# A down projection in block products, and transposes of merged sums with one PSUM bank per pair

## The chip, the cores and the metric

The kernel runs on one core of one Trainium2 chip. The metric is device time in microseconds (us), the median of three runs. Engines are called as the profile calls them: PE (TensorE, matrix products), PEld (its weight loads), DVE (VectorE), ACT (ScalarE), POOL (GpSimd), SP (the queue that issues most DMAs).

## The reference

One layer of a decoder trunk on 256 tokens of width 2048, in float32: a hybrid mixer with a residual, a SwiGLU with a residual, a last norm.

```
m   = g0*(ya @ w_br_a) + g1*(yb @ w_br_b) + g2*(yc @ w_br_c)      # three mixers, gated
h   = x + m @ w_out
f   = rms_norm(h, norm_ffn)
h   = h + (silu(f @ w_gate) * (f @ w_up)) @ w_down                # D_FF = 5632
out = rms_norm(h, norm_final)
```

## The kernel before

Every product is taken in three parts of type float32r. `split` (L105 to L112) cuts a float32 tile into a high part, which ACT writes (L108), and the low remainder, which DVE subtracts (L109). A product is then hi\*hi + lo\*hi + hi\*lo: three matmuls of 128x512. All weights pass through that split on the chip, so every matmul needs one ACT and one DVE pass over its weights first.

Tokens are two tiles of 128 (NT = 2), weights are loaded as 1 MB `raw` tiles. A `Group` (units of class `KTiles`) makes 512 output columns over K in steps of four K-tiles: 24 matmuls a unit. A `Squares` group makes two blocks of 512 columns at once, from pairs of K-tiles. A pair of kind "N" takes eight products (24 matmuls). A pair of kind "W" takes seven (21 matmuls) by a scheme of block sums: its unit "Wp" has 9 matmuls, its unit "Ws" 12, and it needs sums of the weight blocks (L433 to L435 on DVE, into one more slot) and differences of the activation blocks (`differences`, L152 to L173). Seven banks collect the products (numbered 1 to 7): `squares_early` (L455) reads banks 1, 6 and 7 when the last "Ws" is through, `squares_end` (L463 to L471) the others at the end.

SwiGLU has 11 chunks of 512 columns of D_FF, grouped in `PARTS` of 3, 3, 3 and 2. For each chunk `swiglu` runs one `Squares` group (K-pairs of kinds NNWNWNWN, gate and up as the two blocks). Its `finish` takes the results out of PSUM, applies silu (ACT, L941), multiplies (DVE, L944), transposes on PE (L951, four 128x128 into one bank, twice a chunk) and splits the result. After a part, `down` multiplies its 12 (or 8) K-tiles with w_down, one `Group` for each 512 output columns, and adds onto `h` (L986).

The program's order is the order in which the code is written (manual schedule). `run` walks the units. Ahead of a unit it issues the cuts of later units, as long as the slots that these need (N 2, Wp 3, Ws 2) stay within `cap` (9 in these stages); then the unit's matmuls; then one step of a side generator (`beside`): those are `finish`, the transposes and so on. So an engine's queue holds cuts and side steps in one fixed order, and an instruction whose input is late holds up all behind it on its engine. Tiles live in 22 `slots` of 8 KB a partition and in 8 PSUM banks; a new tile waits until its slot or bank was last read.

In the mixer, `br` merges the three gated branches into `m`; its `turn` transposes `m` by `transposed` (L246: two transposes into a bank of their own, one split of 128x256), two calls a step.

Of the kernel before, what the change touches and what calls it, by code (L numbers as in the profile page):

```python
# [13 lines left out]
OP = mybir.AluOpType  # L14
# [19 lines left out]
PARTS = ((0, 3), (3, 6), (6, 9), (9, 11))  # L34
FFN_KINDS = "NNWNWNWN"
GATE_KINDS = "NWNWNWWN"


def bucket_spans():
# [12 lines left out]
def trunk(ctx: ExitStack, tc: tile.TileContext, x, norm_mix, norm_ffn, w_in, w_pool, pool_scale,  # L52
# [64 lines left out]
    class Lazily(dict):  # L117


        def __init__(self, make):  # L120
            self.make = make
# [5 lines left out]
    class Halves:  # L127

        def __init__(self, kinds=None):
# [18 lines left out]
        def differences(self, p, a):  # L150

            e = wk().rearrange("p (n s) -> p n s", s=P)  # L152
            n = 4 if self.kinds[p] == "W" else 2
            if n == 2:
                nc.vector.tensor_tensor(e[:, 0:2], a[:, :, 0], a[:, :, 1], OP.subtract)
            else:
                f = a.rearrange("p k t s -> p (k t) s")
                nc.vector.tensor_tensor(e[:, 0:2], f[:, 1:2].to_broadcast([P, 2, P]), f[:, 0:4:3], OP.subtract)
                nc.vector.tensor_tensor(e[:, 2], f[:, 0], e[:, 1], OP.subtract)
                nc.vector.tensor_tensor(e[:, 3], f[:, 2], e[:, 2], OP.subtract)  # L160
            for i, (tile, used) in enumerate(self.tiles):
                if used + 2 * n <= 16:
                    break
            else:
                i, tile, used = len(self.tiles), late_slot([16, P], F32R), 0
# [11 lines left out]
        def fill(self, p, pt, scales):  # L177

            a = wk()
            for j in range(2):  # L180
                k = slice(j * SEQ, (j + 1) * SEQ)
                nc.scalar.activation(a[:, k], pt[:, k], AF.Copy, scale=scales[j])
            split(*self.pair(p), a.rearrange("p (k s) -> p k s", k=2))
            self.differences(p, a.rearrange("p (k t s) -> p k t s", k=2, t=NT))


    xt = [slot([D_MODEL]) for _ in range(NT)]
# [642 lines left out]
    def br(n, b, plain=False):  # L830
# [13 lines left out]
                m.extend([both[:, i, t] for t in range(NT)] for i in range(2))  # L844

        def turn():
            for j in range(4):
                transposed(mT[0](4 * n + j), [m[n][t][:, j * P:(j + 1) * P] for t in range(NT)])
                if j % 2:
                    yield  # L850

        def after(acc):
            if b == 2 and n == 0:
# [62 lines left out]
        return Group(lambda: mT[0], range(KT), w_out, 0, n * CH, after, before, span=4)  # L916


    act, ready = {}, set()
    gf = []  # L920

    def load_gf():
        gf.append(slot([D_MODEL]))
        nc.sync.dma_start(gf[0], bass.AP(tensor=norm_final.tensor, offset=norm_final.offset,
                                         ap=[[0, P], [1, D_MODEL]]))

    def swiglu(f, last):

# [9 lines left out]
        def finish(b):  # L938
            c = squares_end(b, early[0])
            for t in range(NT):  # L940
                nc.scalar.activation(c[t][0], c[t][0], AF.Silu, scale=rstd2[t])  # L941
            yield
            for t in range(NT):
                nc.vector.scalar_tensor_tensor(c[t][1], c[t][1], rstd2[t], c[t][0], OP.mult, OP.mult)  # L944
            yield
            act[f] = a = slot([8, SEQ], F32R)
            for k in range(2):
                pt = bank()
                for i in range(2):
                    for t in range(NT):  # L950
                        nc.tensor.transpose(pt[:, i * SEQ + t * P:i * SEQ + (t + 1) * P],  # L951
                                            c[t][1][:, (2 * k + i) * P:(2 * k + i + 1) * P], ident)
                split(a[:, 2 * k:2 * k + 2, :], a[:, 4 + 2 * k:6 + 2 * k, :], pair(pt))
                if k == 0:
                    yield
            ready.add(f)

        def before():
            cap[0] = 9

        def after(b):
            beside(finish(b), after=1 if last else 2, lag=1)

        return Squares(lambda: hT[0], load, after, begin, before)

    def down(part, n):
# [2 lines left out]
        cs = cols(n)  # L969

        def lhs():
            def tile(kt):
                assert kt // 4 in ready
                return act[kt // 4][:, kt % 4, :], act[kt // 4][:, 4 + kt % 4, :]
            return tile

        def before():
            if last and n == 0:
# [3 lines left out]
        def after(acc, t=None, c=slice(0, CH)):  # L982
# [7 lines left out]
            if last and n == 2:  # L990
# [2 lines left out]

        return Group(lhs, range(4 * f0, 4 * f1), w_down, f0 * CH, n * CH, after, before, staggered=last and n == 3,
                     span=4)

    def final_norm(acc, t, c):

# [14 lines left out]
        for n in (0, 1, 3, 2):  # L1013
# [2 lines left out]
                nc.vector.tensor_scalar(hn, hn, a[9], None, OP.mult)  # L1016
            else:
                nc.scalar.activation(hn, hn, AF.Copy, scale=a[9])
            (nc.sync if n in (0, 3) else nc.scalar).dma_start(out[toks(t), cols(n)], hn)

    groups = qkv("a", 0, start_block)
    groups += [channels("u", 3 * WIDTH, c, start_pooling if c else None) for c in range(2)]
# [54 lines left out]
```

## Time and profile before

| | |
|---|---|
| median of 3 runs | 1565.94 us (1565.84 to 1566.08) |
| profiled execution | 1565.91 us, of which its span is 1564.1 us |
| PE busy in the span | 1545.4 us (99%) |
| DVE, ACT busy | 1093.8 us (70%), 746.3 us (48%) |
| granted PE clock, mean | 0.996 |
| DMA | 300 MB, mean 192 GB/s |

The profiled execution lies 0.03 us below the median, so durations of its trace can be set against the median as they stand. Busy shares are averages over stages: what a wait costs is read where it stands.

### The profile page before, as it was taken

To read this page: it belongs to the slowest core of one execution; us is meant where nothing else is said; L and a number is where in the kernel's file an instruction comes from. 1 tells how busy PE (TensorE), PEld (TensorE's weight loads), DVE (VectorE), ACT (ScalarE), POOL (GpSimd) and SP (SyncE) were. 2 spreads that over 40 slices of the span, in tenths; PEclk is the share of its full clock that TensorE was granted. 3 is DMA by queue.
4 is the path that set the end of the run, shared out by engine and by line. 5 is a ranking of instruction groups with operands and counts; after the bars stand their busy time and mean duration, and the time that the engine had idled before them with its cause. 6 is when DMAs were issued, how large, how long until landed. Compare 5 with 4: busy or idle time off the path is not lost.

```text
span 1564.1 us, 19170 instructions
## 1 busy us (share of the span) xinstructions
PE 1545.4 (99%) x7895; PEld 1322.9 (85%) x7895; DVE 1093.8 (70%) x1064; ACT 746.3 (48%) x726; POOL 25.9 (2%) x94
## 2 busy tenths in 40 slices
PE   9999999999999999989999999999999999999997
PEld 9998999988888888878888878888888888888886
DVE  6453665644578888867666898667886769857685
ACT  7324343446545544635455545443554345544353
POOL 2000000101100000000000000000000000000000
PEclk9999999999999999999999999999999999999999
DMA  9655455554545655736654566555665555655551
GB/s 352 215 189 165 145 182 176 169 186 137 189 162 191 239 172 205 269 108 244 214 175 163 200 215 215 189 170 181 214 219 190 183 188 189 242 188 164 213 215 54
DMA packets 144456, 300.13 MB, mean 192 GB/s; under 512 B 6464, under 2 KB 8048, under 8 KB 144240
## 3 DMA queue, kind: packets, MB, share of 16 engines
q1 hardware_dynamic: 143024, 296.39, 55.6%
q10 hardware_dynamic: 1040, 1.45, 0.3%
q8 instruction: 62, 1.02, 0.3%
q0 software_dynamic: 304, 1.06, 0.2%
q14 instruction: 26, 0.21, 0.0%
HBM read 296.77 MB, written 2.11 MB: 191 GB/s over the span
## 4 chain that ended last, share of the span: by engine, by line
PE 96%; DVE 2%; ACT 1%; issue 0%; DMA 0%; ACTq 0%; DVEq 0%
PE bank L451 38%; PE bank L344 13%; PE bank L345 13%; PE bank L349 13%; PE bank L364 5%; PE bank L372 5%; PE bank L366 5%; DVE slot L109 1%; PE bank L951 1%; ACT slot L108 1%; PE bank L249 0%; PE bank L596 0%; DMA slot<-in_x_dram 0%; PE bank L597 0%; DVE slot L433 0%
## 5 line engine op out<-in xcount | busy, mean ns | idle before, releaser
L109 DVE TENSOR_TENSOR slot<-slot,slot 128x2048 fp32r<-128x2048 f32 (+3 forms) x406 | 719.0, 1798 | 187.3 <-ACT slot L108 186.8
L108 ACT ACTIVATE slot<-slot 128x2048 fp32r<-128x2048 f32 (+3 forms) x406 | 600.8, 1516 | 339.8 <-DVE slot L435 135.9
L451 PE MATMUL bank<-slot,slot 128*128 128x512 f32 x1719 | 441.3, 391 | 0.0
L451 PEld LDWEIGHTS bank<-slot,slot 128*128 128x128 f32 x1719 | 323.4, 189 | 67.0
L344 PE MATMUL bank<-slot,slot 128*128 128x512 f32 (+1 forms) x936 | 364.4, 390 | 0.0
L345 PE MATMUL bank<-slot,slot 128*128 128x512 f32 (+1 forms) x936 | 362.3, 388 | 0.0
L451 PE MATMUL bank<-slot,late 128*128 128x512 f32 x1014 | 279.4, 390 | 0.0
L349 PE MATMUL bank<-slot,slot 128*128 128x512 f32 (+1 forms) x936 | 236.5, 387 | 0.0
L451 PEld LDWEIGHTS bank<-slot,late 128*128 128x128 f32 x1014 | 189.6, 188 | 39.3 <-DVE slot L109 0.2
L344 PEld LDWEIGHTS bank<-slot,slot 128*128 128x128 f32 x936 | 175.8, 188 | 35.3
L345 PEld LDWEIGHTS bank<-slot,slot 128*128 128x128 f32 x936 | 175.9, 188 | 35.1
L349 PEld LDWEIGHTS bank<-slot,slot 128*128 128x128 f32 x936 | 174.9, 188 | 35.9
L364 PE MATMUL bank<-slot,slot 128*128 128x256 f32 x640 | 158.6, 286 | 0.0
L366 PE MATMUL bank<-slot,slot 128*128 128x256 f32 x640 | 156.9, 283 | 0.0
L366 PEld LDWEIGHTS bank<-slot,slot 128*128 128x128 f32 x640 | 122.8, 192 | 0.0
L364 PEld LDWEIGHTS bank<-slot,slot 128*128 128x128 f32 x640 | 122.7, 192 | 0.1
L372 PE MATMUL bank<-slot,slot 128*128 128x256 f32 x640 | 89.8, 283 | 0.0
L108 ACT ACTIVATE slot<-bank 128x512 fp32r<-128x512 f32 (+1 forms) x46 | 23.3, 520 | 132.0 <-PE bank L951 67.8
L372 PEld LDWEIGHTS bank<-slot,slot 128*128 128x128 f32 x640 | 82.6, 192 | 0.0
L109 DVE TENSOR_TENSOR slot<-bank,slot 128x512 fp32r<-128x512 f32 (+1 forms) x46 | 26.9, 595 | 59.4 <-ACT slot L108 59.4
L433 DVE TENSOR_TENSOR slot<-slot 128x1024 f32<-128x1024 f32 x49 | 59.7, 1218 | 0.0
L986 DVE TENSOR_TENSOR slot<-bank,slot 128x512 f32<-128x512 f32 x30 | 19.6, 686 | 55.5 <-PE bank L349 55.5
(160 smaller groups left out, 630.3 us busy)
## 6 DMA issues: line engine op xcount, KB each, us to landing
slot<-in_w_in_dram SPq DMA_DIRECT2D x103, 1024.0 KB, 5.1
slot<-in_w_gate_dram SPq DMA_DIRECT2D x88, 512.0 KB, 3.9
slot<-in_w_up_dram SPq DMA_DIRECT2D x88, 512.0 KB, 4.8
slot<-in_w_down_dram SPq DMA_DIRECT2D x44, 1024.0 KB, 5.1
slot<-in_w_out_dram SPq DMA_DIRECT2D x16, 1024.0 KB, 5.1
slot<-in_w_br_a_dram SPq DMA_DIRECT2D x8, 1024.0 KB, 5.1
slot<-in_w_br_b_dram SPq DMA_DIRECT2D x8, 1024.0 KB, 5.1
slot<-in_w_br_c_dram SPq DMA_DIRECT2D x8, 1024.0 KB, 5.1
```

What stands on the lines that cost most here:

```text
L108: nc.scalar.activation(hi, src, AF.Copy)
L109: nc.vector.tensor_tensor(lo, src, f32(hi), OP.subtract)
L344: nc.tensor.matmul(acc[:, c], hi[:, toks(t)], whi[:, j, c], start=i + j == 0, stop=False)
L345: nc.tensor.matmul(acc[:, c], lo[:, toks(t)], whi[:, j, c], start=False, stop=False)
L349: nc.tensor.matmul(acc[:, c], hi[:, toks(t)], wlo[:, j, c], start=False, stop=i + j == n - 1)
L364: nc.tensor.matmul(o, whi[:, j, w], hi, start=i + j == 0 and c % 2 == 0, stop=False, skip_group_check=True)
L366: nc.tensor.matmul(o, whi[:, j, w], lo, start=False, stop=False, skip_group_check=True)
L372: nc.tensor.matmul(o, wlo[:, j, w], hi, start=False, stop=i + j == n - 1 and c % 2 == 1, skip_group_check=True)
L433: nc.vector.tensor_tensor(s[:, 0:2], raw[:, 0:1].to_broadcast([P, 2, CH]), raw[:, 1:3], OP.add)
L451: nc.tensor.matmul(g.banks[b], x, w[:, k, :], start=start, stop=g.left[b] == 0)
L951: nc.tensor.transpose(pt[:, i * SEQ + t * P:i * SEQ + (t + 1) * P], c[t][1][:, (2 * k + i) * P:(2 * k + i + 1) * P], ident)
L986: nc.vector.tensor_add(h[t][:, cs], acc[t], h[t][:, cs])
```

## The change

Three things change.

The down projection of the first three parts becomes two `Squares` groups a part (`down_pair`), each with 1024 output columns and K-pairs of kinds NWNWNN. Their results are added onto `h` by nine DVE instructions, straight from the banks. So that the "W" pairs have their operands, `swiglu` now fills the transposed activations through `fill`: ACT copies the bank to SBUF, the split reads that copy, and `differences` makes and splits the block differences of each pair. These differences live in two more slots, and `cap` falls from 9 to 8 in the SwiGLU. The last part keeps `down`.

`turn` puts the four transposes of a pair into one bank and splits 128x512 once, where two banks and two splits of 128x256 stood.

All output DMAs go out on SP's queue, where half of them were ACT's.

```diff
+DOWN_KINDS = "NWNWNN"
...
         def fill(self, p, pt, scales):
             a = wk()
-            for j in range(2):
+            for j in range(2) if scales else ():
...
+            if not scales:
+                nc.scalar.activation(a, pt, AF.Copy)
             split(*self.pair(p), a.rearrange("p (k s) -> p k s", k=2))
             self.differences(p, a.rearrange("p (k t s) -> p k t s", k=2, t=NT))
...
         def turn():
-            for j in range(4):
-                transposed(mT[0](4 * n + j), [m[n][t][:, j * P:(j + 1) * P] for t in range(NT)])
-                if j % 2:
-                    yield
+            for i in range(2):
+                pt = bank()
+                for j in range(4):
+                    c = (2 * i + j // 2) * P
+                    nc.tensor.transpose(pt[:, j * P:(j + 1) * P], m[n][j % 2][:, c:c + P], ident)
+                split(*mT[0].pair(2 * n + i), pt.rearrange("p (k s) -> p k s", k=2))
+                yield
...
-                split(a[:, 2 * k:2 * k + 2, :], a[:, 4 + 2 * k:6 + 2 * k, :], pair(pt))
+                p = 2 * (f - part_of(f)) + k
+                if act[0].kinds:
+                    act[0].fill(p, pt, None)
+                else:
+                    split(*act[0].pair(p), pair(pt))
...
         def before():
-            cap[0] = 9
+            cap[0] = 8
...
+    def down_pair(part, i):
...
+        def finish(b):
+            c12, w, x = early[0]
+            add(0, 0, b[5])
+            add(1, 0, b[5])
+            add(0, 0, b[3])
+            add(0, 1, b[2])
+            add(1, 1, b[4])
+            yield
+            add(0, 0, w)
+            add(0, 1, c12)
+            add(1, 0, x)
+            add(1, 1, x, OP.subtract)
+
+        return Squares(lambda: act[0], load, lambda b: beside(finish(b), after=2, lag=1), begin, None, DOWN_KINDS)
...
-            (nc.sync if n in (0, 3) else nc.scalar).dma_start(out[toks(t), cols(n)], hn)
+            nc.sync.dma_start(out[toks(t), cols(n)], hn)
...
-        k = 2 if f1 - f0 > 2 else 3
-        groups += [tuple(down(part, n) for n in range(k))] + [down(part, n) for n in range(k, D_MODEL // CH)]
+        if part < len(PARTS) - 1:
+            groups += [down_pair(part, i) for i in range(2)]
+        else:
+            groups += [tuple(down(part, n) for n in range(3)), down(part, 3)]
```

Line numbers shift by 14 up to the middle of the file (L109 becomes L110, L451 L465) and by 20 at `swiglu` (L944 becomes L964, L951 L970).

The first place is DVE's queue after a chunk that is followed by another. Before, from the split of the first transposed pair to the next pair's weights (a name ends in the number of its tile; slots of 128x1536 and 128x2048 are the weights of Wp and Ws of the fifth K-pair, 128x1024 and 128x512 their sums):

```order
L109 TENSOR_TENSOR slot_7281<-bank_7282,slot_7281 128x512
L433 TENSOR_TENSOR slot_7291<-slot_7142 128x1024
L434 TENSOR_TENSOR slot_7291<-slot_7291,slot_7142 128x512
L435 TENSOR_TENSOR slot_7291<-slot_7291,slot_7142 128x512
L109 TENSOR_TENSOR slot_7290<-slot_7142,slot_7289 128x1536
L109 TENSOR_TENSOR slot_7298<-slot_7291,slot_7297 128x2048
L109 TENSOR_TENSOR slot_7281<-bank_7318,slot_7281 128x512
```

The same stretch of the change, from the difference of the first pair on:

```order
L157 TENSOR_TENSOR wk_7267<-wk_7262 128x256
L110 TENSOR_TENSOR slot_7269<-wk_7267,slot_7269 128x256
L447 TENSOR_TENSOR slot_7274<-slot_7118 128x1024
L448 TENSOR_TENSOR slot_7274<-slot_7274,slot_7118 128x512
L449 TENSOR_TENSOR slot_7274<-slot_7274,slot_7118 128x512
L110 TENSOR_TENSOR slot_7273<-slot_7118,slot_7272 128x1536
L110 TENSOR_TENSOR slot_7264<-wk_7299,slot_7264 128x512
L160 TENSOR_TENSOR wk_7303<-wk_7299 128x256
L161 TENSOR_TENSOR wk_7303<-wk_7299,wk_7303 128x128
L162 TENSOR_TENSOR wk_7303<-wk_7299,wk_7303 128x128
L110 TENSOR_TENSOR slot_7269<-wk_7303,slot_7269 128x512
L110 TENSOR_TENSOR slot_7310<-slot_7274,slot_7309 128x2048
```

The split of the Ws weights (128x2048) stood ahead of the second transposed pair; now it stands behind that pair's split and its three differences, and two instructions were put ahead of the sums.

The second place is DVE's queue after the last chunk of a part. Before, from the last `squares_early` on (L467 to L471 is `squares_end`, L944 the product whose result PE transposes):

```order
L460 TENSOR_TENSOR wk_7756<-bank_7607,wk_7755 128x512
L109 TENSOR_TENSOR slot_7761<-slot_7695,slot_7760 128x2048
L467 TENSOR_TENSOR wk_7755<-bank_7513,wk_7755 128x512
L468 TENSOR_TENSOR wk_7790<-bank_7513,wk_7756 128x512
L469 TENSOR_TENSOR wk_7755<-bank_7518,wk_7755 128x512
L470 TENSOR_TENSOR wk_7754<-bank_7503,wk_7754 128x512
L471 TENSOR_TENSOR wk_7756<-bank_7508,wk_7756 128x512
L109 TENSOR_TENSOR slot_7799<-slot_7725,slot_7798 128x2048
L944 SCALAR_TENSOR_TENSOR wk_7754<-wk_7754,st_6_103,wk_7755 128x512
L944 SCALAR_TENSOR_TENSOR wk_7756<-wk_7756,st_6_103,wk_7790 128x512
```

And of the change:

```order
L474 TENSOR_TENSOR wk_7756<-bank_7597,wk_7755 128x512
L447 TENSOR_TENSOR slot_7762<-slot_7695 128x1024
L448 TENSOR_TENSOR slot_7762<-slot_7762,slot_7695 128x512
L449 TENSOR_TENSOR slot_7762<-slot_7762,slot_7695 128x512
L110 TENSOR_TENSOR slot_7761<-slot_7695,slot_7760 128x1536
L481 TENSOR_TENSOR wk_7755<-bank_7497,wk_7755 128x512
L482 TENSOR_TENSOR wk_7792<-bank_7497,wk_7756 128x512
L483 TENSOR_TENSOR wk_7755<-bank_7502,wk_7755 128x512
L484 TENSOR_TENSOR wk_7754<-bank_7487,wk_7754 128x512
L485 TENSOR_TENSOR wk_7756<-bank_7492,wk_7756 128x512
L110 TENSOR_TENSOR slot_7801<-slot_7762,slot_7800 128x2048
L964 SCALAR_TENSOR_TENSOR wk_7754<-wk_7754,st_6_103,wk_7755 128x512
```

One split of a weight tile ahead of `squares_end` became three sums and a split. On PE the first transposes of that chunk now stand behind 24 + 9 matmuls of the down projection, before behind 48.

The third place is PE's queue at the third pair of transposes of a `turn` of the mixer. Before:

```order
L249 MATMUL bank_5844<-ident,slot_4028 128x128 [waits DVE_49]
L249 MATMUL bank_5844<-ident,slot_4028 128x128
L249 MATMUL bank_5849<-ident,slot_4028 128x128 [waits DVE_49]
L249 MATMUL bank_5849<-ident,slot_4028 128x128
L451 MATMUL bank_5756<-slot_5750,slot_189 128x512 [waits Activation_49]
```

The same place of the change, from the last matmul ahead of it:

```order
L465 MATMUL bank_5761<-slot_5717,slot_125 128x512
L865 MATMUL bank_5837<-ident,slot_4028 128x128 [waits DVE_49]
L865 MATMUL bank_5837<-ident,slot_4028 128x128 x3
L465 MATMUL bank_5756<-slot_5750,slot_189 128x512 [waits Activation_49]
L465 MATMUL bank_5756<-slot_5750,slot_189 128x512 x3
```

The second wait on DVE, for a second bank, is gone.

## Rows read from the trace of the kernel before

**Rows 1.** The page: busy us (share) xinstructions of two engines; the chain by engine.

```profile
PE 1545.4 (99%) x7895; PEld 1322.9 (85%) x7895; DVE 1093.8 (70%) x1064; ACT 746.3 (48%) x726; POOL 25.9 (2%) x94
PE 96%; DVE 2%; ACT 1%; issue 0%; DMA 0%; ACTq 0%; DVEq 0%
```

**Rows 2.** Waits of PE from 100 us on: total us, times, longest us.

```profile
PE bank L249 <- DVE slot L109: 6.1, 2, 5.2
PE bank L951 <- DVE wk L944: 1.2, 2, 0.8
```

**Rows 3.** Timeline of PE, down projection: start, us, engine, line, operation, count.

```profile
1000.78 1.98 PE L349 MATMUL bank<-slot,slot 128*128 128x512 f32 x8
...
1006.23 1.98 PE L349 MATMUL bank<-slot,slot 128*128 128x512 f32 x8
```

**Rows 4.** Busy us by engine of one whole part: PE, PEld, DVE, ACT, POOL, clock, DMA.

```profile
1095.08:1287.68 192.60, 192.60 (x862) 159.45 (x861) 144.67 (x113) 88.71 (x60) 0.00 (x0) 1.00 0.58 197
```

**Rows 5.** Timeline of PE, mixer, around its longest wait.

```profile
691.53 0.38 PE L249 MATMUL bank<-ident,slot 128*128 128x128 f32 x2
697.09 0.69 PE L249 MATMUL bank<-ident,slot 128*128 128x128 f32 x2 [5.18 <-DVE slot L109]
...
708.46 0.44 PE L249 MATMUL bank<-ident,slot 128*128 128x128 f32 x2 [0.93 <-DVE slot L109]
...
711.27 0.39 PE L451 MATMUL bank<-slot,slot 128*128 128x512 f32 x1
```

**Rows 6.** Stretches within and after that wait; the clock is third from the end.

```profile
694.50:695.00 0.50, 0.00 (x0) 0.00 (x0) 0.50 (x1) 0.15 (x1) 0.00 (x0) 1.00 0.00 0
697.00:701.00 4.00, 3.91 (x11) 3.14 (x12) 1.43 (x3) 2.18 (x2) 0.00 (x0) 0.50 0.33 136
```

**Rows 7.** Timeline of PE and ACT at a chunk's first transposes.

```profile
1137.51 0.60 PE L951 MATMUL bank<-ident,wk 128*128 128x128 f32 x4
1137.86 1.41 PE L451 MATMUL bank<-slot,late 128*128 128x512 f32 x5
...
1138.14 0.60 ACT L108 ACTIVATE slot<-bank 128x512 fp32r<-128x512 f32 x1 [4.63 <-PE bank L951]
```

**Rows 8.** Timeline of DVE from a chunk's end to the next weights.

```profile
1128.45 0.68 DVE L467 TENSOR_TENSOR wk<-bank,wk 128x512 f32<-128x512 f32 x1
...
1133.55 2.29 DVE L109 TENSOR_TENSOR slot<-slot,slot 128x2048 fp32r<-128x2048 f32 x1 [2.02 <-ACT slot L108]
1135.76 1.41 DVE L944 SCALAR_TENSOR_TENSOR wk<-wk,st,wk 128x512 f32<-128x512 f32 x2
...
1139.38 1.22 DVE L433 TENSOR_TENSOR slot<-slot 128x1024 f32<-128x1024 f32 x1
...
1141.97 1.75 DVE L109 TENSOR_TENSOR slot<-slot,slot 128x1536 fp32r<-128x1536 f32 x1
```

**Rows 9.** Timeline of DVE, output projection: a fill with differences (W, then N).

```profile
830.46 0.69 DVE L109 TENSOR_TENSOR slot<-wk,slot 128x512 fp32r<-128x512 f32 x1 [1.51 <-ACT slot L108]
...
832.84 0.69 DVE L109 TENSOR_TENSOR late<-wk,late 128x512 fp32r<-128x512 f32 x1 [0.70 <-ACT late L108]
834.64 2.29 DVE L109 TENSOR_TENSOR slot<-slot,slot 128x2048 fp32r<-128x2048 f32 x1 [1.11 <-ACT slot L108]
...
837.45 0.42 DVE L155 TENSOR_TENSOR wk<-wk 128x256 f32<-128x256 f32 x1
838.35 0.42 DVE L109 TENSOR_TENSOR late<-wk,late 128x256 fp32r<-128x256 f32 x1 [0.48 <-ACT late L108]
```

**Rows 10.** Timeline of DVE at the end of a chunk: splits in a row, then squares_early.

```profile
1153.76 8.90 DVE L109 TENSOR_TENSOR slot<-slot,slot 128x2048 fp32r<-128x2048 f32 x4 [0.38 <-ACT slot L108]
1162.57 0.68 DVE L459 TENSOR_TENSOR wk<-bank,wk 128x512 f32<-128x512 f32 x1
```

**Rows 11.** Output DMAs by queue: count, KB each, median us from issue to landing.

```profile
out_dram<-slot SPq DMA_DIRECT2D x4, 256.0 KB, 2.6
out_dram<-slot ACTq DMA_DIRECT2D x4, 256.0 KB, 3.4
```

More of the change, by code (lines that the diff above doesn't have):

```diff
@@ L127, in trunk, with __init__ @@
     class Halves:
-        def __init__(self, kinds=None):
+        def __init__(self, kinds=None, take=None):
+            self.take = take or late_slot
             self.parts = Lazily(lambda: slot([4, 2, SEQ], F32R))
@@ L164, in differences @@
             else:
-                i, tile, used = len(self.tiles), late_slot([16, P], F32R), 0
+                i, tile, used = len(self.tiles), self.take([16, P], F32R), 0
                 self.tiles.append(None)
@@ L179, in fill, with __call__, pair @@
             a = wk()
-            for j in range(2):
+            for j in range(2) if scales else ():
                 k = slice(j * SEQ, (j + 1) * SEQ)
                 nc.scalar.activation(a[:, k], pt[:, k], AF.Copy, scale=scales[j])
+            if not scales:
+                nc.scalar.activation(a, pt, AF.Copy)
             split(*self.pair(p), a.rearrange("p (k s) -> p k s", k=2))
             self.differences(p, a.rearrange("p (k t s) -> p k t s", k=2, t=NT))
+    class Chunks(Halves):
+        def __call__(self, kt):
+            return self.parts[kt // 4][:, kt % 4, :], self.parts[kt // 4][:, 4 + kt % 4, :]
+        def pair(self, p):
+            k = p % 2 * 2
+            return self.parts[p // 2][:, k:k + 2, :], self.parts[p // 2][:, 4 + k:6 + k, :]
     xt = [slot([D_MODEL]) for _ in range(NT)]
@@ L916, in output @@
         return Group(lambda: mT[0], range(KT), w_out, 0, n * CH, after, before, span=4)
-    act, ready = {}, set()
+    act = {}
     gf = []
@@ L925, in load_gf, with part_of @@
                                          ap=[[0, P], [1, D_MODEL]]))
+    def part_of(f):
+        return max(f0 for f0, _ in PARTS if f0 <= f)
     def swiglu(f, last):
@@ L945, in finish @@
             yield
-            act[f] = a = slot([8, SEQ], F32R)
             for k in range(2):
@@ L952, in finish @@
                                             c[t][1][:, (2 * k + i) * P:(2 * k + i + 1) * P], ident)
-                split(a[:, 2 * k:2 * k + 2, :], a[:, 4 + 2 * k:6 + 2 * k, :], pair(pt))
+                p = 2 * (f - part_of(f)) + k
[3 more added lines that the diff above has]
+                    split(*act[0].pair(p), pair(pt))
                 if k == 0:
                     yield
-            ready.add(f)
         def before():
-            cap[0] = 9
+            cap[0] = 8
         def after(b):
+            if f == part_of(f):
+                act[0] = Chunks(DOWN_KINDS if f < PARTS[-1][0] else None, slot)
+                act[0].parts = Lazily(lambda: slot([8, SEQ], F32R))
             beside(finish(b), after=1 if last else 2, lag=1)
@@ L971, in lhs @@
         def lhs():
[L972 to L975, printed above, removed]
+            a = act[0]
+            return lambda kt: a(kt - 4 * f0)
         def before():
@@ L995, in down, with load, begin, add @@
                      span=4)
+    def down_pair(part, i):
+        f0 = PARTS[part][0]
+        n0 = 2 * i
+        def load(raw, p):
+            r = f0 * CH + 2 * p * P
+            nc.sync.dma_start(raw.rearrange("p j n c -> p j (n c)"),
+                              w_down[r:r + 2 * P, n0 * CH:(n0 + 2) * CH].rearrange("(j p) c -> p j c", p=P))
+        early = []
+        def begin(b):
+            early.append(squares_early(b))
+        def add(t, n, x, op=OP.add):
+            hn = h[t][:, cols(n0 + n)]
+            nc.vector.tensor_tensor(hn, hn, x, op) if op == OP.subtract else nc.vector.tensor_tensor(hn, x, hn, op)
+        def finish(b):
[11 more added lines that the diff above has]
+        return Squares(lambda: act[0], load, lambda b: beside(finish(b), after=2, lag=1), begin, None, DOWN_KINDS)
     def final_norm(acc, t, c):
```

## Prediction

> **What bounds the kernel now.** I read four views. The first is the page: PE is busy for 99% of the span and is 96% of the chain that ended last, DVE is at 70% [rows 1]. So time goes only with matmuls taken out or with a wait of PE. The second view is PE's waits: after the first 100 us two places are left, 6.1 us at the mixer's transposes and 1.2 us at the transposes of the SwiGLU, the only price that the transposes have [rows 2]. The third is the timeline of PE: a unit of 24 matmuls takes 1006.23 - 1000.78 = 5.45 us, so a matmul costs 0.227 us wherever PE doesn't wait [rows 3]. The fourth is one whole part, three chunks and their down projection: 192.60 us, in which PE is never idle and DVE is busy for 144.67 us, so DVE has 48 us free [rows 4]. This change buys matmuls with DVE's work, so the question is whether those 48 us lie where the work falls due.
>
> **Gain: matmuls.** A down projection of 6 pairs and 1024 columns had 144 matmuls and gets 4 x 24 + 2 x 21 = 138. With two halves a part and three parts, 36 go, at 0.227 us [rows 3]: -8.2 us.
>
> **Gain: transposes in the mixer.** PE's third pair of transposes waited 5.18 us, because its bank was still being read by a split that stood in DVE's queue behind a large weight split; the fourth waited 0.93 us [rows 5]. The clock was granted at 1.00 up to the wait and at 0.50 after it, 1.2 instead of 2.4 GHz [rows 6], so that 4 us or so of matmuls went at half speed. From 691.53 us to the end of the last row, about 711.5, there are 20.0 us. The same work at full speed is four pieces of transposes, which the new order joins to two of 0.35 us, and 45 matmuls: 0.7 + 45 x 0.227 = 10.9 us. In the new order one bank serves four transposes, so the third wait's bank is one whose split stands a unit earlier, not behind the fresh split. I take the whole: -9.05 us. Its bounds are 0 (the wait comes back at the next weights, which hang on the same DVE) and -9.05.
>
> **Gain: the wait of 1.2 us** at a chunk's first transposes [rows 2]: in the new order the product that PE waits for stands one large split earlier in the queue after the first chunk: -1.2.
>
> **Cost: DVE's work.** Per part two halves with two W pairs add weight sums of 2.6 us (1139.38 to 1141.97, [rows 8]) and turn one 128x2048 split of 2.2 us a unit [rows 10] into one of 1.7 and one of 2.2: near 26 us; the differences of six pairs add some 7. DVE comes to 177 of about 190 us, 93%. On average that fits, but its queue has one order, and it has to fit at each place.
>
> **Cost inside a part (twice a part, six times).** This is the first place of the order. Count from the first transposes of a chunk. PE then has 45 matmuls (12, 24 and 9) and two blocks of transposes of 0.35 us [rows 7] ahead of the Ws unit of its fifth K-pair: 10.9 us. On the other side stands one chain. The bank is read by ACT 0.63 us after the transposes begin, the copy takes 0.6 [rows 7]; high part and remainder of the pair take about 0.6 each, the difference with its split 0.9 [rows 9], and with 0.35 for handing over this stands at 3.8 us. The weight sums (2.6) end at 6.4 and the 128x1536 split (1.7) at 8.05 [rows 8]. Then comes the second pair, of kind W: from its split to the Ws weights whose high part ACT could cut only behind the differences, 4.18 us in the mixer's output projection (830.46 to 834.64, [rows 9]). So the Ws high part is ready at 12.2 us: PE waits 1.3 us; the remainder of 2.29 us comes at 14.5, when PE is through with its eight high-part products after 1.8: another 0.45. I take 1.75 us each, +10.5 in all. Bounds: nothing, if ACT cuts the Ws high part before the differences reach it, to 2.8 us, if the waits of ACT (1.51 in [rows 9]) add to it, so 0 to +17.
>
> **Cost from the last chunk into the down projection (three times).** This is the second place. Before, the product that PE transposes was ready 8.7 us after the end of the chunk: from 1128.45 the first product starts at 1135.76 and two end at about 1137.2 [rows 8], and PE bridged this with 48 matmuls (10.9 us). Now the transposes come after 33 (24 and 9), or 7.5 us. This alone is 1.2 us of wait. DVE must besides be on time: it enters the end of the chunk with, from the Ws split at 12.2 us on, two splits (4.4), sums and split (4.3), three splits (6.6), the early reading of banks (1.3) and once more sums and split (4.3) [rows 8, 10], with 0.35 for a wait on ACT: 33.4 us, where PE, through with the chunk's remaining matmuls, stands at 31.05. So DVE is 2.4 us late and the wait is 2.4 + 8.7 - 7.5 = 3.6 us. A second wait follows at the Ws weights of the fourth pair of the down projection, by the same kind of chain as inside a part, which I put a little shorter at 1.3. I take 4.9 each, +14.7. Bounds: 1.2 to 6.5 each, 3.6 to 19.5. From one half of the down projection to the next and into the next part I find no wait: the banks come free before their pair needs them.
>
> **No cost.** The merged transposes save ACT and DVE work beside PE. The last part has no W pairs and keeps its code. At the very end all outputs go on one queue: SP's land in 2.6 us and ACT's in 3.4 [rows 11], so the last one may land 0.8 earlier, or, queued behind its neighbours, 0.8 later; I take 0.
>
> **Sum**, against the profiled execution's 1565.91 us, 0.03 below the median: -8.2 - 9.05 - 1.2 + 10.5 + 14.7 = +6.75, so 1572 to 1573; I take 1572. A part would take 192.60 - 2.7 + 8.4 = 198.3 us.
>
> **Rivals.**
> *DVE keeps pace* (first rival). DVE is free for 48 us of a part [rows 4], and the entries into my two sums are 1.3 and 2.4 us of lateness against 12 and 33 us of chain; a few short hand-overs decide. If the Ws high part is ready within 10.9 us of the transposes, and the end of the chunk is on time, what remains is 3 x (1.2 + about 1) and a few short waits, some 7.5 us: 1565.9 - 18.45 + 7.5 = 1555. Against it: DVE at 93% with a fixed order.
> *The clock falls as well* (second). This is slower still. After the wait of 5.18 us the clock was at 0.50 [rows 6], and that cost 9.05 - 6.11 = 2.9 us beyond the waits themselves. If the 3.6 us at the end of a chunk do the same, three times some 2.2 us come on top: 1572.5 + 6.6, about 1579. It decides when DVE arrives at the end of the chunk 1 or 2 us later still. For it: my 3.6 us lies nearer to 5.18 than to 0.93. Against it: no row shows the clock after a wait of such a length.
> The Trainium skill (TensorE: Matmul & The Clock Gate, HAM oscillation — how this bites in real kernels) says that a matmul kernel whose engine idles again and again for the operands of its next tile loses its clock again after each gap. The trace agrees for the one long wait, 1.00 before and 0.50 after [rows 6]; by that page the sum would be the second rival's, about 1579.
> *The mixer's wait moves* (third). The split that held the bank also ends ahead of the next weights' remainder; if PE waits there as long, -9.05 falls away: 1572.5 + 9, about 1581. Against it: the remainders that come next are due a unit later.
>
> **How the numbers follow.** What this measurement can tell from no change is 0.2%, 1562.8 to 1569.1. My forecast holds 0.48, with a range of its own from 1566 to 1577 by the bounds of the two costs; the first rival 0.30; the second 0.13; the third 0.09. Of the forecast's 0.48 some 0.16 lies below 1569.1, of the first rival's 0.30 some 0.05 above 1562.8: same 0.21. Faster is the rest of the first, 0.25, and 0.01 of lucky ends: 0.26. Slower: 0.53. The range is 1554 to 1580, since both signs hold weight; it leaves out the better tail of the first and most of the third.
>
> **What would show it.** The transposes of the third chunk of a part waiting some 3.6 us for the SwiGLU's product, three times; matmuls of the Ws unit of a chunk's fifth pair waiting 1 to 2 us for ACT's high part or DVE's remainder, six times; no wait left at the mixer's transposes, with a clock of 1.00 from 691 to 712 us; 198 us from part to part. I am wrong if a part takes about 190 us (DVE kept pace), if it takes over 200 with the clock at 0.50 in it (second rival), or if the mixer waits about 5 us at a weight instead of at a transpose (third).

## The result, and the profile after

The change makes the kernel slower: 1576.63 us (median of six runs, 1575.57 to 1577.39) against 1565.89 (1565.35 to 1566.19), a ratio of 1.0068 with a 95% interval of 1.0055 to 1.0081, or 10.7 us. The profiled execution of the change took 1577.39 us, its span 1575.7, so it lies 0.76 us above the median.

The page of the change (busy us, share, count by engine), which answers to [rows 1]: 36 matmuls fewer, and PE yet busy for longer, with a share of 98%; DVE works 90 us more.

```profile
PE 1547.1 (98%) x7859; PEld 1317.7 (84%) x7859; DVE 1184.2 (75%) x1194; ACT 782.4 (50%) x772; POOL 25.9 (2%) x94
PE 86%; DVE 7%; issue 3%; ACT 2%; DMA 1%; ACTq 0%; DVEq 0%; SPq 0%
```

PE's waits from 100 us on (total us, times, longest us), which answer to [rows 2]. The waits at the two old places are gone; three new groups have 17.3 us.

```profile
PE bank L970 <- DVE wk L964: 9.1, 6, 2.8
PE bank L465 <- ACT slot L109: 6.1, 6, 1.1
PE bank L465 <- DVE slot L110: 2.1, 7, 0.8
```

Where they stand is read from the timeline of PE (start, us, line, count, idle time before). First transposes of chunks, which are the marks of the ledger below (894.42 and 981.13 are the first and third chunk of part 1; 1093.78, 1137.99 and 1180.02 the three of part 2; then the first of parts 3 and 4):

```profile
894.42 0.88 PE L970 MATMUL bank<-ident,wk 128*128 128x128 f32 x4
...
981.13 0.33 PE L970 MATMUL bank<-ident,wk 128*128 128x128 f32 x1 [2.75 <-DVE wk L964]
...
1093.78 0.60 PE L970 MATMUL bank<-ident,wk 128*128 128x128 f32 x4
...
1137.99 0.84 PE L970 MATMUL bank<-ident,wk 128*128 128x128 f32 x4
...
1180.02 0.33 PE L970 MATMUL bank<-ident,wk 128*128 128x128 f32 x1 [2.71 <-DVE wk L964]
1180.69 0.90 PE L970 MATMUL bank<-ident,wk 128*128 128x128 f32 x3 [0.33 <-DVE wk L964]
...
1292.44 0.60 PE L970 MATMUL bank<-ident,wk 128*128 128x128 f32 x4
...
1492.37 0.60 PE L970 MATMUL bank<-ident,wk 128*128 128x128 f32 x4
```

And the same marks of the kernel before that were not shown yet:

```profile
901.87 0.33 PE L951 MATMUL bank<-ident,wk 128*128 128x128 f32 x1 [0.85 <-DVE wk L944]
...
1177.91 0.60 PE L951 MATMUL bank<-ident,wk 128*128 128x128 f32 x4
...
1287.68 0.60 PE L951 MATMUL bank<-ident,wk 128*128 128x128 f32 x4
...
1480.28 0.60 PE L951 MATMUL bank<-ident,wk 128*128 128x128 f32 x4
```

| stretch | before | after | difference |
|---|---|---|---|
| start to first transposes | 901.87 | 894.42 | -7.45 |
| part 1 | 193.21 | 199.36 | +6.15 |
| part 2 | 192.60 | 198.66 | +6.06 |
| part 3 | 192.60 | 199.93 | +7.33 |
| from there to the end of the span | 83.8 | 83.3 | -0.5 |
| sum | 1564.1 | 1575.7 | +11.6 |

Part 2 in pieces: first to second chunk 42.43 before ([rows 4, 7] give 1095.08 and 1137.51) and 44.21 after, +1.78. Second to third chunk 40.40 before; 15 matmuls fewer stand ahead of the third chunk's transposes (3.4 us), with +1.78 that would be 38.8, and it is 42.03: 3.25 us more. Of these the wait ahead of the third chunk's transposes has 2.87 (2.71 drawn and 0.16 that is not, see below); the rest lies in the second chunk, whose own waits are longer (1.08 us at its fifth pair, 0.84 instead of 0.60 for its transposes). Third chunk to the next part 109.77 before; with those 3.4 back and 12 matmuls fewer (2.7) it would be 110.45, and it is 112.42: +1.97. These come to 1.78 x 2 + 3.25 + 1.97 = 8.78, less 2.72 for the matmuls: +6.06.

The wait of 1.78 is seen at the Ws unit of the fifth pair (PE, DVE and ACT together; the Ws high part is the first of the three in the second of ACT's lines):

```profile
1103.20 0.29 DVE L162 TENSOR_TENSOR wk<-wk,wk 128x128 f32<-128x128 f32 x1
1103.53 0.63 ACT L109 ACTIVATE slot<-wk 128x512 fp32r<-128x512 f32 x1 [3.81 <-DVE wk L162]
...
1104.07 5.08 ACT L109 ACTIVATE slot<-slot 128x2048 fp32r<-128x2048 f32 x3
...
1106.02 1.66 PE L465 MATMUL bank<-slot,late 128*128 128x512 f32 x6 [0.92 <-ACT slot L109]
...
1108.34 0.98 PE L465 MATMUL bank<-slot,late 128*128 128x512 f32 x3 [0.21 <-DVE slot L110]
```

ACT waits 3.81 us for the last difference (L162), cuts it, and only then begins with the Ws weights at 1104.07; PE has been ready since 1105.10. A matmul that follows another starts 0.227 us after it, but its busy time is drawn as 0.39, so each wait costs some 0.16 more than the idle time shown. The first matmuls behind a wait are slower as well: the rows that follow these two start at 1107.51 and 1109.16, so six matmuls took 1.49 us and three 0.82, where 1.36 and 0.68 would do. Idle 0.92 + 0.21, undrawn 0.32 and these 0.27 are 1.72 of the 1.78.

The end of the third chunk on DVE, which answers to [rows 8]:

```profile
973.04 0.68 DVE L481 TENSOR_TENSOR wk<-bank,wk 128x512 f32<-128x512 f32 x1
...
978.12 2.29 DVE L110 TENSOR_TENSOR slot<-slot,slot 128x2048 fp32r<-128x2048 f32 x1 [2.02 <-ACT slot L109]
980.33 1.41 DVE L964 SCALAR_TENSOR_TENSOR wk<-wk,st,wk 128x512 f32<-128x512 f32 x2
```

This is part 1. PE asks for the transposes at 981.13 - 2.75 = 978.4; its chunk ended 33 matmuls (7.5 us) earlier, at 970.9, and DVE begins to read its banks at 973.04, 2.1 us late; the product is ready 8.7 us later. What the wait leaves behind stands in the windows (PE busy, PEld, DVE, ACT, POOL, granted clock, DMA share, GB/s); the last row is a whole part, for [rows 4]:

```profile
1180.00:1184.00 4.00, 3.64 (x11) 2.93 (x12) 3.86 (x4) 1.25 (x3) 0.00 (x0) 0.57 0.00 0
...
1380.00:1384.00 4.00, 4.00 (x12) 3.13 (x11) 3.43 (x5) 2.58 (x4) 0.00 (x0) 0.50 0.00 0
1384.00:1388.00 4.00, 4.00 (x19) 3.22 (x18) 3.93 (x5) 1.67 (x3) 0.00 (x0) 0.86 0.35 93
...
1093.78:1292.44 198.66, 193.20 (x850) 157.91 (x849) 175.10 (x159) 100.86 (x78) 0.00 (x0) 0.99 0.56 191
```

The levels are 1.00 and 0.50 (2.4 and 1.2 GHz). In part 2 PE was busy for 3.64 us at a mean of 0.57, which loses (1 - 0.57) x 3.64 = 1.6 us of work; with the second wait of 0.33 this is nearly all of the 1.97. In part 3, after a wait as long, 0.50 and 0.86 over 8 us lose 2.6: this is why that part is 1.3 us longer than part 2. Why the clock stayed down for longer there is not shown.

The mixer, for [rows 5]: the third and fourth transposes have no idle time before them, and the Ws unit's twelve matmuls follow at full rate.

```profile
692.04 0.60 PE L865 MATMUL bank<-ident,slot 128*128 128x128 f32 x4
692.40 3.01 PE L465 MATMUL bank<-slot,slot 128*128 128x512 f32 x12
...
700.01 0.60 PE L865 MATMUL bank<-ident,slot 128*128 128x128 f32 x4
700.37 1.63 PE L465 MATMUL bank<-slot,late 128*128 128x512 f32 x6
```

With 12 matmuls behind 700.37 this stretch ends at 703.1: 11.1 us, 8.9 less than before. The granted clock is 1.00 from 691 to 712 us.

### The profile page after: what moved, and what is told of

It reads as the page before. It is cut to its first block, busy times and chain, and to the rows that moved or that the text cites. A ratio compares the mean times of both kernels' runs of the same rounds, so it can differ in the third digit from the quotient of the medians.

```text
span 1575.7 us, 19336 instructions
## 1 busy us (share of the span) xinstructions
PE 1547.1 (98%) x7859; PEld 1317.7 (84%) x7859; DVE 1184.2 (75%) x1194; ACT 782.4 (50%) x772; POOL 25.9 (2%) x94
## 4 chain that ended last, share of the span: by engine, by line
PE 86%; DVE 7%; issue 3%; ACT 2%; DMA 1%; ACTq 0%; DVEq 0%; SPq 0%
PE bank L465 41%; PE bank L358 9%; PE bank L359 9%; PE bank L363 9%; PE bank L378 5%; PE bank L386 5%; PE bank L380 5%; DVE slot L110 4%; ACT slot L109 2%; DVE slot L447 1%; DVE wk L964 1%; DVE slot L448 1%; PE bank L610 0%; PE bank L970 0%; DMA slot<-in_x_dram 0%
## 5 line engine op out<-in xcount | busy, mean ns | idle before, releaser
L110 DVE TENSOR_TENSOR slot<-slot,slot 128x2048 fp32r<-128x2048 f32 (+3 forms) x418 | 738.0, 1796 | 178.3 <-ACT slot L109 178.3
L109 ACT ACTIVATE slot<-slot 128x2048 fp32r<-128x2048 f32 (+3 forms) x418 | 614.3, 1513 | 266.5 <-DVE slot L449 132.1
L465 PE MATMUL bank<-slot,slot 128*128 128x512 f32 x2547 | 634.5, 392 | 0.9 <-DVE slot L110 0.8
L465 PEld LDWEIGHTS bank<-slot,slot 128*128 128x128 f32 x2547 | 480.3, 189 | 102.1 <-DVE slot L110 1.3
L465 PE MATMUL bank<-slot,late 128*128 128x512 f32 x1014 | 282.0, 392 | 7.4 <-ACT slot L109 6.1
L358 PE MATMUL bank<-slot,slot 128*128 128x512 f32 (+1 forms) x648 | 251.7, 389 | 0.0
L359 PE MATMUL bank<-slot,slot 128*128 128x512 f32 (+1 forms) x648 | 250.2, 387 | 0.0
L465 PEld LDWEIGHTS bank<-slot,late 128*128 128x128 f32 x1014 | 188.6, 188 | 51.1 <-ACT slot L109 8.7
L363 PE MATMUL bank<-slot,slot 128*128 128x512 f32 (+1 forms) x648 | 165.4, 386 | 0.0
L447 DVE TENSOR_TENSOR slot<-slot 128x1024 f32<-128x1024 f32 x61 | 74.2, 1216 | 0.0
L961 ACT ACTIVATE wk<-wk,st 128x512 f32<-128x512 f32 x22 | 14.7, 716 | 95.5 <-DVE wk L483 95.5
L110 DVE TENSOR_TENSOR slot<-wk,slot 128x512 fp32r<-128x512 f32 (+1 forms) x44 | 27.1, 616 | 27.3 <-ACT slot L109 27.2
L109 ACT ACTIVATE slot<-bank 128x512 fp32r<-128x512 f32 x20 | 12.0, 598 | 70.4 <-PE bank L865 30.1
```

The lines of the kernel that those rows point to most:

```text
L109: nc.scalar.activation(hi, src, AF.Copy)
L110: nc.vector.tensor_tensor(lo, src, f32(hi), OP.subtract)
L358: nc.tensor.matmul(acc[:, c], hi[:, toks(t)], whi[:, j, c], start=i + j == 0, stop=False)
L359: nc.tensor.matmul(acc[:, c], lo[:, toks(t)], whi[:, j, c], start=False, stop=False)
L363: nc.tensor.matmul(acc[:, c], hi[:, toks(t)], wlo[:, j, c], start=False, stop=i + j == n - 1)
L447: nc.vector.tensor_tensor(s[:, 0:2], raw[:, 0:1].to_broadcast([P, 2, CH]), raw[:, 1:3], OP.add)
```

## The experiments

Each ratio is against the kernel before, run beside it, with its 95% interval.

**The transposes of the mixer alone** (the function `turn` of the change in the kernel before):

```diff
-                transposed(mT[0](4 * n + j), [m[n][t][:, j * P:(j + 1) * P] for t in range(NT)])
...
+                split(*mT[0].pair(2 * n + i), pt.rearrange("p (k s) -> p k s", k=2))
```

> The kernel before with the merged transposes of the mixer alone; down projection and output queues as before. My theory: the 5.18 and 0.93 us waits and the half-speed clock behind them go, 20.0 us of that stretch become 10.9, so 1565.9 - 9 = 1557, and no PE wait over 0.5 us at 690 to 712 us. Rival (the wait moves to the next weights): 1565 to 1566, with a wait of about 5 us at a matmul for DVE's remainder.

Measured: 1556.87 us, 0.9941 (0.9925 to 0.9958). The only waits of PE left from 100 us on are the old ones of the SwiGLU; the second line is its first transposes, 8.95 us earlier than the 901.87 of the kernel before.

```profile
PE bank L954 <- DVE wk L947: 1.2, 2, 0.9
...
892.92 0.33 PE L954 MATMUL bank<-ident,wk 128*128 128x128 f32 x1 [0.86 <-DVE wk L947]
```

The mixer's part of the change is worth its 9 us. It is the fastest kernel of this study, faster than before and change. The rest of the change, the down projection with its cap and the one output queue, thus costs 1576.6 - 1556.9 = 19.7 us on top, though it has 36 matmuls (8.2 us) fewer.

**The product early.** In the last chunk of a part the products are issued behind silu without a step in between:

```diff
-            yield
+            early_product = last and act[0].kinds
+            if not early_product:
+                yield
...
-            yield
+            yield 2 if early_product else 1
```

> The changed kernel, except that in the last chunk of a part with a block-product down projection the two products that PE transposes are issued right behind silu, ahead of the next Ws weight split in DVE's queue; PE's order is the same. My theory (the wait of 3.1 us at the third chunk's transposes comes from that split, which itself waits about 2 us for ACT, and the half-speed clock follows the wait): the product is done near 977.7 us instead of 981.7, before PE asks at 978.4; 3 x (3.2 + about 2) = 15.6 us less, 1561, and the clock at 1.00 after the chunk. Rival (DVE has too much work in a part, so the wait moves to the next weights of the down projection): over 1572, with new waits for DVE's remainder there.

Measured: 1573.32 us, 1.0047 (1.0032 to 1.0061); 3.3 us were won of 15.6. The rival was right in that the wait moves: the product is in time, but PE waits some 11 us later, for ACT's high part of Ws weights of the down projection (the rival had named DVE's remainder).

```profile
977.61 0.60 PE L972 MATMUL bank<-ident,wk 128*128 128x128 f32 x4
...
991.33 13.90 PE L465 MATMUL bank<-slot,slot 128*128 128x512 f32 x53 [2.22 <-ACT slot L109]
```

```profile
992.00:996.00 4.00, 4.00 (x12) 3.05 (x11) 4.00 (x3) 4.00 (x3) 0.00 (x0) 0.57 0.42 130
```

Here too the clock falls, to a mean of 0.57, after 2.22 us of idle time.

**The differences late.** `fill` only copies and splits; the differences follow one and two units later:

```diff
+            for p, a in todo:
+                yield
+                act[0].differences(p, a.rearrange("p (k t s) -> p k t s", k=2, t=NT))
```

> The changed kernel, except that the differences of a chunk's two pairs are made and split one and two units after the second transposes, not in between; the sum of the work is the same. My theory (the Ws weights of the fifth pair are late because ACT's high part of them stands behind that of the differences): the six pairs of waits of 1.1 and 0.2 us go, 6 x 1.78 = 10.7 us less, 1566. Rival (it is DVE's total of the work in the chunk, which is not less): waits of the same size turn up one or two units later, 1574 to 1577.

Measured: 1582.51 us, 1.0102 (1.0085 to 1.0119), slower by 6 us than the change. The waits at the fifth pair's Ws unit are gone, so the differences ahead of its weights do cause them; but there are new ones at the next weights and at the transposes of the second chunk (0.56 us), and the one at the third chunk grew:

```profile
1116.79 0.73 PE L467 MATMUL bank<-slot,slot 128*128 128x512 f32 x2 [0.45 <-DVE slot L110]
...
1182.62 0.48 PE L973 MATMUL bank<-ident,wk 128*128 128x128 f32 x1 [3.82 <-DVE wk L967]
```

**Both of these.**

> The products early and the differences late, together. My theory: the two kinds of wait are independent, 1576.6 - 15.6 - 10.7 = 1550, faster than before by about 1%. Rival (one DVE, too much work): well above the sum of the two single gains, 1560 or more.

Measured: 1575.05 us, 1.0058 (1.0043 to 1.0073). My theory of two independent waits falls: what is taken from one place turns up at the next, here at a bank that waits for the additions onto `h`:

```profile
1012.01 8.24 PE L467 MATMUL bank<-slot,slot 128*128 128x512 f32 x28 [2.40 <-DVE slot L1045]
```

**No W pairs in the down projection:**

```diff
-DOWN_KINDS = "NWNWNN"
+DOWN_KINDS = "NNNNNN"
```

(with the parts of `finish` left out that read the banks of W pairs).

> The changed kernel with all six pairs of the down projection of kind N (no weight sums, no Ws splits, differences of N pairs alone; 36 matmuls more than with two W pairs, as many as before the change). My theory now (DVE has no slack around the chunks, so moved work only moves the wait, and only less work helps): nearly all waits go, 1556 to 1560, as with the merged transposes alone (1556.9). Rival (the way through the copy and the differences is what delays the chunks, not the W work): waits of 1 us at the fifth pair and 2 us or more at the third chunk stay, 1570 or more.

Measured: 1564.84 us, 0.9996 (0.9986 to 1.0005). Neither: the large waits at the third chunk are gone, which W pairs at the second and fourth place thus cause, but it is 8.0 us above the transposes alone with as many matmuls. The first part takes 195.52 us (893.49 to 1089.01), with DVE busy for 152.34; in the second, which begins at 1089.01, the first transposes of the other two chunks stand here:

```profile
1132.32 0.89 PE L971 MATMUL bank<-ident,wk 128*128 128x128 f32 x4
...
1174.04 0.87 PE L971 MATMUL bank<-ident,wk 128*128 128x128 f32 x4
```

PE's waits at the fifth pairs are short (at most 0.3 us each), but with what is not drawn and the transposes (0.89 instead of 0.60) the way from chunk to chunk is 43.31 and 41.72 us where 42.43 and 40.40 stood before: 0.88 and 1.32, some 2.4 a part with what follows the third chunk. The change has 1.78 at the first of these places and some 2.2 at the second, so half or more of that comes with what N pairs need too: the copy, the differences and their slots.

**One W pair:** `DOWN_KINDS = "NNNWNN"`.

> The changed kernel with one W pair in six (the fourth pair, NNNWNN): 18 matmuls (4.1 us) more than the change, half of its sums and Ws splits, and 48 matmuls ahead of the third chunk's transposes. My theory: the waits at the third chunk go, those in the second chunk stay (3 x 1.8 = 5.4), 1557 - 4.1 + 5.4 = 1558. Rival (half the work is enough to keep DVE late): waits of 2 us or more in all parts, 1565 or more.

Measured: 1563.37 us, 0.9986 (0.9977 to 0.9996): 1.6 us below the rival's 1565 and 5.4 above the theory. By the waits the theory is right: there is none at the third chunk, one of 1.1 at the fifth pair behind the fill of kind W, and one of 0.24 behind that of kind N, which I had put at nothing.

**The sums on POOL:**

```diff
+                e = nc.gpsimd if self.g.pool else nc.vector
```

> The changed kernel with the weight sums of the W pairs of the down projection made by POOL instead of DVE (the SwiGLU's stay on DVE): DVE has 2.6 us less per W pair, 10.4 us a part. My theory: DVE comes to the end of the third chunk about 2 us earlier, so the wait there and the half-speed clock behind it go in most part, 1566 to 1570; the waits at the fifth pair stay. Rival (POOL's sums are slow or slow DVE down): 1576 or more, with the Ws weights of the down projection waiting for POOL.

Measured: 1586.23 us, 1.0131 (1.0114 to 1.0148): the rival's time, but not by its waits: PE waits for no sum of POOL, and its waits at the third chunk grow from 9.1 to 17.1 us. The product on DVE took 4.50 us instead of 1.41 while POOL was adding (first two rows: DVE; last: POOL):

```profile
977.36 2.29 DVE L110 TENSOR_TENSOR slot<-slot,slot 128x2048 fp32r<-128x2048 f32 x1 [2.02 <-ACT slot L109]
979.57 4.50 DVE L965 SCALAR_TENSOR_TENSOR wk<-wk,st,wk 128x512 f32<-128x512 f32 x2
```

```profile
977.38 4.47 POOL L448 TENSOR_TENSOR slot<-slot 128x1024 f32<-128x1024 f32 x1 [3.88 <-PE bank L466]
```

The Trainium skill (SBUF — State Buffer, 🔬 SBUF: two separate sides) has it that a DVE instruction with two SBUF inputs and one of GpSimd that reads SBUF lock each other out for a whole instruction; these rows agree. The split that began at 977.36 kept its 2.29 us and the sum beside it took 4.47; the product that began inside that sum ended behind it.

**The kernel before again**, as a measure of what can be told apart.

> The kernel before once more, on the same chip as the three others: 1566, no difference.

Measured: 1565.50 us, 1.0002 (0.9992 to 1.0011).

**The cap alone** (`cap[0] = 8` in the SwiGLU of the kernel with the merged transposes).

> The kernel before with the merged transposes (1556.9) and cap 8 instead of 9 in the SwiGLU, nothing else. If the lower cap by itself delays the fifth pair's weights behind the second transposed pair: 6 to 11 waits of about 0.2 to 0.4 us and 1560 to 1566. If only the copy and the differences do (a plain pair is short enough): 1557, no such wait.

Measured: 1558.03 us, 0.9958 (0.9941 to 0.9974), 1.2 us above the kernel with cap 9 by the medians and 2.7 by the ratios, which lie within each other's intervals. No wait at a fifth pair; one appears at the first weights of the SwiGLU, which the change has as well (862.21 us), and the first transposes come 1.6 us later than the 892.92 with cap 9:

```profile
862.28 0.73 PE L451 MATMUL bank<-slot,slot 128*128 128x512 f32 x2 [0.84 <-DVE slot L109]
...
894.50 0.88 PE L954 MATMUL bank<-ident,wk 128*128 128x128 f32 x4
```

From there on a part takes 192.6 to 192.9 us, much as before. So the lower cap by itself costs some 1.5 us, at this one place; the waits at the fifth pairs do not come without the copy and the differences.

**The change with cap 9.**

> The changed kernel with cap 9, so that the Ws weights of the fifth pair are cut ahead of the second transposed pair, as before the change. My theory: the six waits of 1.1 and 0.2 us (1.78 each with what they push) go, 10.7 us; DVE then comes to the end of the third chunk about as late, so the wait there stays: 1566. Rival one (slots: with two slots more in use a cut waits for a slot, and the waits turn up as late weights elsewhere): 1573 or more. Rival two (DVE's total): 1570 to 1576, as with the late differences.

Measured: 1595.99 us, 1.0197 (1.0182 to 1.0213), the slowest. By time it is in the first rival's range (1573 or more), but the largest waits are not at late weights, where that rival had them. The Ws weights come in time at the fifth pair; instead the transposes of each second and third chunk wait, for some 3.2 and 4.4 us:

```profile
PE bank L970 <- DVE wk L964: 25.6, 14, 4.4
```

With cap 9 a Ws split stands ahead of the reading of the banks at the chunk's end: its row (930.47, before L481 at 932.68) has no counterpart there with cap 8.

```profile
930.47 2.29 DVE L110 TENSOR_TENSOR slot<-slot,slot 128x2048 fp32r<-128x2048 f32 x1 [0.38 <-ACT slot L109]
932.68 0.68 DVE L481 TENSOR_TENSOR wk<-bank,wk 128x512 f32<-128x512 f32 x1
```

**Cap 9 and the W pairs third and fifth.**

> The changed kernel with cap 9 and the W pairs third and fifth (NNWNWN): as many matmuls and as much work for DVE, but 48 matmuls ahead of the third chunk's transposes, as before the change, where there are 33 in NWNWNN. My theory (cover decides at that place): no wait over 1 us at the transposes and no half-speed clock, 1550 to 1556. Rival (DVE has too much work, whatever the cover): a wait of 2 us or more at the down projection's Ws weights instead, 1562 or more.

Measured: 1578.51 us, 1.0088 (1.0073 to 1.0103); not as expected: 19.2 us of waits at the transposes, where the run before has 25.6, and none of 2 us at the down projection's weights, which the rival had named. But it is 17.5 us faster than the same with NWNWNN.

**The W pairs third and fifth alone:** `DOWN_KINDS = "NNWNWN"`, cap 8.

> The changed kernel (cap 8) with the W pairs third and fifth (NNWNWN) instead of second and fourth: the same matmuls and work for DVE, but 48 matmuls instead of 33 ahead of the third chunk's transposes. If the missing cover costs the wait there: no wait over 1 us at these transposes, no half-speed clock, only the waits at the fifth pair (six of 1.4 to 1.8 us) and 1558 to 1562. If DVE's total decides, whatever the cover: a wait of 2 us or more at the down projection's weights instead, 1566 or more.

Measured: 1565.81 us, 1.0001 (0.9991 to 1.0010), 10.8 us faster than the change with the same matmuls and the same work. The transposes of the third chunk don't wait. In their place PE waits 0.27 us for ACT's high part and 1.33 for DVE's remainder (1.60 us idle) in the down projection, so not the 2 us of the rival; the time lies at its edge. The order moves two things at once, though. There are 48 matmuls of cover instead of 33, and the three sums and the 128x1536 split, which stood ahead of the reading of the banks, now stand behind it: DVE begins to read 0.5 us after PE turns to the down projection (1164.99), where it was 2.1 us late in the change. The product is still 8.7 us behind that.

```profile
1164.99 11.04 PE L465 MATMUL bank<-slot,slot 128*128 128x512 f32 x48
1165.45 0.69 DVE L481 TENSOR_TENSOR wk<-bank,wk 128x512 f32<-128x512 f32 x1
...
1172.70 1.41 DVE L964 SCALAR_TENSOR_TENSOR wk<-wk,st,wk 128x512 f32<-128x512 f32 x2
...
1175.88 0.60 PE L970 MATMUL bank<-ident,wk 128*128 128x128 f32 x4
...
1190.43 9.76 PE L465 MATMUL bank<-slot,slot 128*128 128x512 f32 x41 [1.33 <-DVE slot L110]
```

The cover is worth 15 x 0.227 = 3.4 us and DVE's earlier reading 1.6. The wait in the change was some 2.9 us, so by this arithmetic the cover alone would be enough and the earlier reading alone would not; no run tried them apart.

## Why the prediction was right, point by point

Slower was forecast, at 1572 with 1566 to 1577 as its own range; it is 1576.6. The direction and the two mechanisms that carry it, at the places named, came out; 1572 is 4.6 us short. That the third chunk's 14.7 us came near the 16.1 measured is luck: one of its two waits did not come, and a lower clock stood in for it. In the ledger's terms +6.75 was forecast (-8.2 - 9.05 - 1.2 + 10.5 + 14.7), and the profiled execution has -8.2 - 8.95 + 1.5 + 11.6 + 16.1 - 0.5 = +11.6, where 16.1 is 8.7 and 7.4, as below. The range of 1566 to 1577 does not follow from the stated bounds either: 0 to 17 and 3.6 to 19.5 us on top of the gains give 1551 to 1584.

- Matmuls: right in the count, and a part of the change holds the 2.7 us (the ledger closes with it).
- Transposes in the mixer: -9.05 forecast; -9.2 by the run with them alone, -8.95 by its trace. The third rival, that the wait moves, is out.
- The wait of 1.2 us: gone, but no gain, and the term that was furthest off. The lower cap delays the first weights of the SwiGLU (a wait of 0.83 us and shorter ones that are not drawn), which I had not worked out: the first transposes come at 894.42, 1.5 us later than the 892.92 with the mixer's transposes alone. The run with the cap alone has 894.50. So the term is +1.5 instead of -1.2.
- DVE's work: 175 us a part, forecast 177, but of 199 us instead of 190; and the 177 is luck. By the rows of the forecast four W pairs add 4 x (2.6 + 1.7) = 17 us, not 26, and 17.4 were measured; the ten additions onto `h` and four early readings that come on top, some 9 us, were left out.
- Inside a part: 1.75 forecast; 1.6 to 1.8 measured from the first chunk to the second and some 2.2 from there to the third, 11.6 in all, by the chain that was named (ACT's high part behind the differences): 12.2 us from the transposes to the Ws weights forecast, 12.24 measured (1093.78 to 1106.02). The cap is not enough to explain it, as the run with cap 8 alone shows; the run without W pairs has half of it or more.
- The third chunk: DVE late by 2.4 forecast and 2.1 measured, 8.7 from the banks to the product in both, 3.6 of wait forecast and 3.4 measured (2.71 and 0.33 drawn, with 0.16 more each); ahead of the three marks it is 8.7 us in all.
- The other step that failed is the second wait of 1.3 at the down projection's Ws weights, 3.9 us in all. It did not appear; the first wait covers it, and it is laid bare when the first is taken away (2.22 us in the run with early products). In its place came the half-speed clock: behind the third chunk's transposes the three parts lose 2.20, 1.97 and 3.23 us against the 110.45 of the ledger, 7.4 in all, of which the wait for the second product has at most 0.5 a part; the second rival put 2.2 a part. It came at 3.1 us of wait; I had let it decide only at 1 or 2 us more. So the time lies between the forecast and that rival's 1579. The Trainium skill (TensorE: Matmul & The Clock Gate, HAM oscillation — how this bites in real kernels) describes a kernel whose TensorE waits for the operands of each next tile and starts every tile at the low clock. The rows agree for these three waits, with 0.57 and 0.50 behind them in parts 2 and 3; behind the waits of 0.92 and 1.08 us at the fifth pairs the clock stayed at 1.00.
- The first rival, DVE keeping pace, is out: 17.3 us of waits.
- The output queue: -0.5 from the last part's first transposes to the end, within my 0.8. Every run that has it takes 83.3 to 83.6 us there, every run without it 83.8 to 83.9; it was not tried by itself.

What carries the loss: against 1556.9 with the transposes alone, the same block products cost 8.9 us with the W pairs third and fifth, and 19.7 with them second and fourth. So order has 10.8 of it, by the cover and by what stands ahead of the reading of the banks. Of the rest the run without W pairs shows 8.0 for all else that the change adds: copies, differences with their slots, and the cap, which has some 1.5 by itself. W pairs then add 1.0, which is within the intervals of these runs, although they take 8.2 us of matmuls away; so their weight work costs about 9, as an estimate. That no order of this work is without waits was not shown; six were tried, and each left or moved some.

## What to carry to other kernels

A busy share of 70% on the helper engine is no reserve where a chunk ends: count, for each product that PE will ask for, the work that stands ahead of it in its queue against the matmuls that cover it. Removing matmuls also removes cover, so place the cheap units where nothing is waited for. And where one wait is cured, look for the next one that it covered before counting the gain.

## What the runs showed of the hardware

- PE's clock fell after idle times of 2.22 us and of 2.7 us, as shown, and stayed at 1.00 after one of 1.33 us (first line: W pairs third and fifth, where it ends at 994.90). The length of one idle time does not decide it: the clock stayed at 1.00 after 3.15 us with cap 9 and the same W pairs (the other lines), and in the run with both, early products and late differences, it fell after 2.40 us at 1012.01 (0.69 from 1014 to 1018) and stayed at 1.00 after 2.35 at 1211.65:

```profile
996.00:1000.00 4.00, 4.00 (x19) 3.10 (x18) 4.00 (x3) 4.00 (x3) 0.00 (x0) 1.00 0.94 292
...
939.50 0.33 PE L970 MATMUL bank<-ident,wk 128*128 128x128 f32 x1 [3.15 <-DVE wk L964]
...
940.00:944.00 4.00, 3.84 (x21) 3.23 (x22) 1.72 (x5) 1.48 (x3) 0.00 (x0) 1.00 0.77 256
```

- POOL needed 3.86 us in the mean for a 128x1024 float32 sum beside a busy DVE, where DVE takes 1.22 [rows 8], and while POOL added, DVE's product of two SBUF operands took three times as long (above). The group of POOL's first sums (count, busy us, mean ns, idle time before):

```profile
L448 POOL TENSOR_TENSOR slot<-slot 128x1024 f32<-128x1024 f32 x12 | 46.3, 3862 | 909.1 <-DVE slot L110 862.2 <-PE bank L466 23.6 <-DMA slot<-in_w_down_dram 17.1
```
